# Softmax scale folded into the query copies, minima as biases, head norms by twos, and a new spread of the modulation products, in a two-layer hybrid attention kernel

## The chip, the cores and the metric

The kernel runs on one core of a Trainium2 chip. The metric is the device time of one execution in microseconds (us). The engines are PE (TensorE, matmul), DVE (VectorE), ACT (ScalarE), POOL (GpSimd) and SP (SyncE, which issues the DMAs here). Each engine takes its own instructions in the order in which they stand in its queue and waits where an operand is not there yet.

## The reference

Two trunk layers work on 640 tokens (512 latent, 128 context) of width 1024, all in float32. What is computed in each layer, cut to what matters here:

```python
mod = silu(cond) @ ada_w + ada_b                   # two conditions: context, latent
shift, scale, gate = split(mod, 3)
h = rmsnorm(x, norm_g) * (1 + scale) + shift
c_q, c_kv, k_rope, cb, cc, cx, dq, dk, dv, z = split(h @ w_in)
# latent attention, 4 heads: softmax((q . k) * 96**-0.5) @ v, low-rank q and k, v
# short convolution:         cb * conv3(cc * cx)
# differential attention, 4 heads with two softmax maps of width 64 each:
s = einsum(q, k) * 64 ** -0.5                      # q, k with rotary positions
p = softmax(s)
o = rmsnorm((p[0] - lam * p[1]) @ v, subln) * (1 - lambda_init)
mix = concat(o_mla, o_conv, o_diff) * silu(z)
x = x + gate * (mix @ w_out)
```

Latent queries see 512 latent and 128 cached context keys; context queries see the 128 context keys alone. A final norm and the keys and values of the context tokens are outputs too.

## The kernel before, in words

Activations lie transposed (features on partitions, 640 tokens along the free side) and are worked on in two halves of 320 tokens, j = 0 and 1. A float32 matmul is done as three matmuls over a high and a low part of each operand (`mm3`, lines 362 to 364: high x high, high x low, low x high). The low parts are subtractions on DVE (`mx` L274 for the output projection, `hl` L394 for the layer's input, `klz` L573, `plm` L905 and others) or, for some weights, on POOL (`wli`, L326).

Inside a layer, four sources of work are advanced in step, and the kernel's Python code writes them out in that order; a scheduler then sets each engine's queue from this program order and from what is ready. `main()` yields the projections of the layer one piece at a time; `units()` yields the attention, one unit for each head and block of 128 queries (u = 4 is the context block, then 0 to 3), first the four differential heads, then the four latent (MLA) heads; `bg` holds small jobs (splitting weights, rotary positions); `side()` yields the modulation products. `adv(n)` takes n pieces of `main()`, counts them in `cnt`, and takes one piece of `side()` whenever `cnt` is over a start value and divisible by a step.

**Attention unit (differential, L604 to L650).** PE writes the scores of both maps into PSUM (`S`, two buffers of two banks each, L614). DVE takes the maximum of each row (L624) and multiplies it by minus the scale (L625). ACT computes exp(scale x score + bias) with the row sums (`E`, L631). DVE takes a reciprocal (L633), builds the factor of the second map (L634) and subtracts the maps (L636). PE transposes the result (`tpd`, L594), ACT copies it back (L596), PE multiplies with the values (`O`, L645). The MLA unit is alike with one map (L886, L887, L889, L891, L892). Query copies out of PSUM are ACT copies (L530 for the differential queries, L807 for the latent ones). After a head, `diff_norm` (L651 to L662) takes its five root mean squares in ten small DVE operations of 128x5 (L655 on, `rsqrt`) and one of 128x640 (L661).

**Modulation products.** `mod` needs a matrix-vector product for two conditions. One piece of `ada_cols` (L144) loads 128 rows of the transposed weights (`at`, 256 KB, DMA issued by SP) and runs two DVE multiply-reduce operations over 128x512 (`jk`, L153), each with a short read of its sum. The vector silu(cond), half of it at a time, lies broadcast in a single buffer `cb2`; `silu_bcast` (L134) fills it by two DMAs, a tanh on ACT (L140) and two DVE operations (L141, L142). In layer 0, `side()` has 48 pieces: step 0 the first half of layer 0's gate; step 1 the second half of that gate and of layer 1's shift and scale; step 2, after a new broadcast, the first half of layer 1's shift and scale. Step 2 is 32 products. In layer 1 there are 16 pieces, 32 products, for its gate.

**Output projection (`out_half`, L1149).** Sixteen halves (eight output tiles, two token halves), each of eight steps of three matmuls. In the order of the code: tiles 0 to 3 with both halves, tiles 4 to 7 with the first half, then everything left of `side()`, then the norm of the first half (`y_n`, L203), the second half of tiles 4 and 5, and, between the second halves of tiles 6 and 7, the modulated input of the next layer (`t`, L373, on DVE; `hh`, L390, on ACT; `hl`, L394). The first matmuls of layer 1 (`p1qk`) read `hh` and `hl`, and `t` reads layer 1's scale, `mod_1`.

The two places that set the spread of the products before:

```python
QD, QM, SIDE0 = 5, 3, 18
C1, C2 = 44, 126
SIDES = (8, 4, 5)
...
                cnt[0] += 1
                if cnt[0] > SIDE0 and cnt[0] % SIDES[0 if cnt[0] < C1 else 1 if cnt[0] < C2 else 2] == 0:
                    next(sg, None)
...
                if m % 2 == 0:            # in out_half, for m in range(8)
                    next(sg, None)
```

## Time and profile before

| what | value |
| --- | --- |
| three timed runs | 832.89, 837.35, 837.39 us (median 837.35) |
| the profiled execution, its own time | 832.23 us |
| its span in the trace | 830.2 us |
| PE busy | 783.8 us, 94% |
| DVE busy | 633.4 us, 76% |
| ACT busy | 445.8 us, 54% |
| POOL busy | 70.0 us, 8% |
| mean granted TensorE clock | 0.992 |

The span is the part of the execution that the trace covers; 2.0 us lie around it. A busy share is a mean over stages: layer 0's attention runs from about 80 to 374 us, its output projection to 433, layer 1's attention to 759, and its output projection to the end. The rows below are read stage by stage.

### The profile page before, as it was taken

The page shows a single profiled execution, that of the slowest core. Times are in us where ns is not written, and L with a number is a line of the kernel's source. Part 1 is how long each engine was busy: PE and PEld are TensorE (multiplying, and loading weights), DVE is VectorE, ACT ScalarE, POOL GpSimd, SP SyncE. Part 2 cuts the span into 40 slices and gives each one's busy share as a digit, 9 for nine tenths or more (in the row PEclk, how much of TensorE's full clock was granted, in tenths as well). Part 3 has the DMA queues.
Part 4 walks back from the last instruction along what each step waited for, and adds up shares of the span by engine and source line. Part 5 has one row for each costly group of instructions (what it writes and reads, how often), then busy time and mean ns, then how long its engine had stood idle before and what let it go on. Part 6 is the DMA issues. An engine that isn't in the chain of part 4 may idle for free.

```text
span 830.2 us, 14320 instructions
## 1 busy us (share of the span) xinstructions
PE 783.8 (94%) x5390; PEld 739.3 (89%) x5390; DVE 633.4 (76%) x1494; ACT 445.8 (54%) x978; POOL 70.0 (8%) x45
## 2 busy tenths in 40 slices
PE   6999999989999899999999999999999899999994
PEld 1389988989999888999999998899999899899994
DVE  4788989989998778789567778987778556668535
ACT  2255447454747667674334545546557667756310
POOL 3300011030001102000220002003000200200000
PEclk9999999999999999999999999999999999999997
DMA  8916434132420322135620433411111001111503
GB/s 311 386 66 197 131 104 135 44 92 71 157 83 27 107 90 83 45 120 184 240 102 22 154 103 109 143 30 58 51 59 52 26 26 52 51 53 50 179 1 126
DMA packets 66164, 85.52 MB, mean 103 GB/s; under 512 B 4976, under 2 KB 47408, under 8 KB 66096
## 3 DMA queue, kind: packets, MB, share of 16 engines
q1 hardware_dynamic: 65520, 83.96, 30.9%
q8 instruction: 42, 0.69, 0.3%
q10 hardware_dynamic: 576, 0.66, 0.2%
q14 instruction: 26, 0.21, 0.1%
HBM read 78.14 MB, written 6.46 MB: 102 GB/s over the span
## 4 chain that ended last, share of the span: by engine, by line
PE 60%; DVE 18%; ACT 9%; DMA 7%; issue 3%; POOL 1%; SPq 1%; POOLq 0%; DVEq 0%; ACTq 0%
PE wo L363 5%; PE wo L362 4%; PE wo L364 4%; DVE jk L153 4%; DVE sm L624 2%; ACT E L631 2%; PE O L645 2%; PE p1c L362 2%; PE p1c L364 2%; PE p1c L363 2%; PE tpm L900 2%; PE p1qk L363 2%; PE p1qk L362 2%; PE S L614 2%; PE p1qk L364 2%
## 5 line engine op out<-in xcount | busy, mean ns | idle before, releaser
L153 DVE CUSTOM_DVE_ANT_0 jk<-at,cb 128x512 bf16<-128x512 f32 x128 | 91.9, 718 | 4.9 <-DMA at<-in_adaT 4.2
L631 ACT ACTIVATE E<-S,sm 128x640 f32<-128x640 f32 (+1 forms) x80 | 56.0, 706 | 61.4 <-DVE sm L625 43.3
L363 PE MATMUL wo<-mx,who 128*128 128x320 f32 x256 | 79.3, 311 | 0.1
L364 PE MATMUL wo<-mx,wlo 128*128 128x320 f32 x256 | 79.0, 309 | 0.0
L362 PE MATMUL wo<-mx,who 128*128 128x320 f32 x256 | 78.5, 310 | 0.0
L624 DVE TENSOR_REDUCE sm<-S 128x1 f32<-128x640 f32 (+1 forms) x80 | 55.3, 711 | 3.4 <-PE S L615 2.4
L889 ACT ACTIVATE Em<-Sm,smm 128x640 f32<-128x640 f32 (+1 forms) x40 | 28.3, 708 | 41.9 <-DVE smm L887 40.5
L236 ACT ACTIVATE sqn<-xn 128x320 f32<-128x320 f32 x32 | 15.1, 471 | 64.8 <-DVE xn L1164 64.5
L363 PEld LDWEIGHTS wo<-mx,who 128*128 128x128 f32 x256 | 48.1, 188 | 0.8 <-DVE mx L274 0.6
L614 PE MATMUL S<-kh,qs 128*128 128x320 f32 x128 | 40.7, 327 | 8.5 <-ACT E L631 8.4
L364 PEld LDWEIGHTS wo<-mx,wlo 128*128 128x128 f32 x256 | 48.1, 188 | 0.0
L362 PEld LDWEIGHTS wo<-mx,who 128*128 128x128 f32 x256 | 47.8, 188 | 0.0
L362 PE MATMUL v<-whi_dv,hh 128*128 128x272 f32 x160 | 46.3, 289 | 0.0
L363 PE MATMUL v<-wli_dv,hh 128*128 128x272 f32 x160 | 46.0, 288 | 0.0
L364 PE MATMUL v<-whi_dv,hl 128*128 128x272 f32 x160 | 46.0, 288 | 0.0
L645 PE MATMUL O<-v,atd 128*128 128x128 f32 x336 | 44.1, 275 | 0.2 <-ACT atd L596 0.2
L1164 DVE SCALAR_TENSOR_TENSOR xn<-wo,mod,xn 128x320 f32<-128x320 f32 (+2 forms) x48 | 19.6, 435 | 31.2 <-PE wo L364 21.4
L645 PEld LDWEIGHTS O<-v,atd 128*128 128x128 f32 x336 | 42.1, 192 | 0.5 <-ACT atd L596 0.5
L363 PE MATMUL p0qk<-hl,whi_qk 128*128 128x320 f32 x128 | 40.2, 315 | 2.4 <-DVE hl L394 2.4
L326 POOL TENSOR_TENSOR wli_c<-ri_c,whi_c 128x1024 fp32r<-128x1024 f32 x8 | 19.8, 2475 | 264.7 <-PE p0zm L363 85.4
L362 PE MATMUL p1c<-hh,whi_c 128*128 128x320 f32 x128 | 41.6, 325 | 0.0
L362 PE MATMUL p0c<-hh,whi_c 128*128 128x320 f32 x128 | 41.2, 322 | 0.0
(377 smaller groups left out, 2660.6 us busy)
## 6 DMA issues: line engine op xcount, KB each, us to landing
at<-in_adaT SPq DMA_DIRECT2D x64, 256.0 KB, 4.0
ada<-in_adaA SPq DMA_DIRECT2D x32, 256.0 KB, 5.1
ri_qk<-in_wi SPq DMA_DIRECT2D x16, 512.0 KB, 4.8
ri_c<-in_wi SPq DMA_DIRECT2D x16, 512.0 KB, 4.0
ro<-in_wo SPq DMA_DIRECT2D x16, 512.0 KB, 4.4
ri_dv<-in_wi SPq DMA_DIRECT2D x8, 544.0 KB, 4.6
ri_zd<-in_wi SPq DMA_DIRECT2D x8, 512.0 KB, 3.7
x<-in_xT SPq DMA_DIRECT2D x16, 160.0 KB, 4.8
```

The source lines that it names most:

```text
L153: V.tensor_tensor_reduce(out=junk, in0=raw, in1=cb2[:, c, :], scale=1.0, scalar=0.0, op0=ALU.mult, op1=ALU.add, accum_out=acc)
L326: eng.tensor_tensor(out=lo, in0=raws[hf], in1=hi.bitcast(F32), op=ALU.subtract)
L362: TE.matmul(ps, ah, bh, start=first, stop=False)
L363: TE.matmul(ps, ah, bl, start=False, stop=False)
L364: TE.matmul(ps, al, bh, start=False, stop=last)
L614: TE.matmul(ps[:, j, 0:HB], qs[:, a, qc], kh[:, a, js], start=True, stop=False)
L624: V.tensor_reduce(out=sm[:, a:a + 1], in_=Sv[a], axis=AX.XY if u < 4 else AX.X, op=ALU.max)
L631: S.activation(ev, Sv[a], AF.Exp, bias=sm[:, 2 + a:3 + a], scale=DIFF_SCALE, accum_out=so)
L645: TE.matmul(po[:, 0:128], at[:, c * 128:(c + 1) * 128], vv[:, h * 128:(h + 1) * 128], start=c == 0, stop=c == n - 1)
L889: S.activation(e if u < 4 else e[:, 0:128], Sv, AF.Exp, bias=sm[:, 1:2], scale=MLA_SCALE, accum_out=sm[:, 2:3])
L900: TE.transpose(tp[:, c * 128:(c + 1) * 128], toktile(e, c), ident)
L1164: V.scalar_tensor_tensor(out=xn[kt][:, a:e], in0=ps[:, a - j * HB:e - j * HB], scalar=mod[l][2][:, kt, c:c + 1], in1=xn[kt][:, a:e], op0=A ...
```

## The change: what it does

1. **Scale.** The copies of the query projections out of PSUM (L530, L807 of before) become ACT activations with scale = -(softmax scale). The scores then have the other sign: DVE takes the minimum, ACT computes exp(-score + minimum). The multiplications L625 and L887 (40 each) go. L634 takes a column of `neglam` as a tensor operand in place of a scalar operand.
2. **Head norms by twos.** The sums of two heads lie side by side and `diff_norm` runs once for both: ten small operations of 128x10 instead of twice ten of 128x5. The output tile of the even head waits for that of the odd one. `flush` finishes at most one head at a time.
3. **Spread.** While attention runs, a piece of `side()` is taken when `cnt` is over 18 and divisible by 10 in layer 0, over 128 and divisible by 10 in layer 1. In the output projection one piece is taken for each half (m == 0) in place of four. What is left is drained at the same place in the code, after the twelfth half.

DVE's queue goes from 1476 instructions to 1356; the numbers of matmuls, ACT and POOL instructions and DMAs stay. The diff, without the parts that only rename:

```diff
-    QD, QM, SIDE0 = 5, 3, 18
-    C1, C2 = 44, 126
-    SIDES = (8, 4, 5)
+    QD, QM = 5, 3
+
+    SIDES = ((18, 10), (128, 10))
...
+        def copy(dst, src, scale=None):
+            if scale is None:
+                S.copy(dst, src)
+            else:
+                S.activation(dst, src, AF.Copy, scale=scale)
...
-            res["qr"] = q = yield from proj_raw(nm, 0)
+            res["qr"] = q = yield from proj_raw(nm, 0, -DIFF_SCALE)
...
             for a in range(2):
-                V.tensor_reduce(out=sm[:, a:a + 1], in_=Sv[a], axis=AX.XY if u < 4 else AX.X, op=ALU.max)
-            V.tensor_scalar(out=sm[:, 2:4], in0=sm[:, 0:2], scalar1=-DIFF_SCALE, scalar2=None, op0=ALU.mult)
+                V.tensor_reduce(out=sm[:, a:a + 1], in_=Sv[a], axis=AX.XY if u < 4 else AX.X, op=ALU.min)
...
-                S.activation(ev, Sv[a], AF.Exp, bias=sm[:, 2 + a:3 + a], scale=DIFF_SCALE, accum_out=so)
+                S.activation(ev, Sv[a], AF.Exp, bias=sm[:, a:a + 1], scale=-1.0, accum_out=so)
...
-            V.tensor_scalar(out=sm[:, 7:8], in0=s0[:, u:u + 1], scalar1=sm[:, 6:7], scalar2=neglam[:, l:l + 1],
-                            op0=ALU.mult, op1=ALU.mult)
+            V.scalar_tensor_tensor(out=sm[:, 7:8], in0=s0[:, k5:k5 + 1], scalar=sm[:, 6:7], in1=neglam[:, l:l + 1],
+                                   op0=ALU.mult, op1=ALU.mult)
...
-        def diff_norm(h, acc):
+        def diff_norm(h, oss, ss, s0):
...
-            V.scalar_tensor_tensor(out=e[:, 5:10], in0=ss[:, 0:5], scalar=1.0 / 128, in1=e[:, 0:5], op0=ALU.mult,
+            V.scalar_tensor_tensor(out=e[:, 10:20], in0=ss[:, 0:10], scalar=1.0 / 128, in1=e[:, 0:10], op0=ALU.mult,
                                    op1=ALU.add)
-            y = rsqrt(e[:, 5:10], 5, "d" + tg)
-            ov = os_.rearrange("p (u d) -> p u d", u=5)
-            V.tensor_tensor(out=ov, in0=ov, in1=y.unsqueeze(2).to_broadcast([P, 5, P]), op=ALU.mult)
-            return os_
+            y = rsqrt(e[:, 10:20], 10, "d" + tg)
+            for k, os_ in enumerate(oss):
+                ov = os_.rearrange("p (u d) -> p u d", u=5)
+                V.tensor_tensor(out=ov, in0=ov, in1=y[:, 5 * k:5 * k + 5].unsqueeze(2).to_broadcast([P, 5, P]),
+                                op=ALU.mult)
...
-                    S.copy(qp[m][:, js], ps)
+                    copy(qp[m][:, js], ps, -MLA_SCALE)
...
-            V.tensor_reduce(out=sm[:, 0:1], in_=Sv, axis=AX.XY if u < 4 else AX.X, op=ALU.max)
-            V.tensor_scalar(out=sm[:, 1:2], in0=sm[:, 0:1], scalar1=-MLA_SCALE, scalar2=None, op0=ALU.mult)
+            V.tensor_reduce(out=sm[:, 0:1], in_=Sv, axis=AX.XY if u < 4 else AX.X, op=ALU.min)
...
-                if cnt[0] > SIDE0 and cnt[0] % SIDES[0 if cnt[0] < C1 else 1 if cnt[0] < C2 else 2] == 0:
+                if cnt[0] > SIDES[l][0] and cnt[0] % SIDES[l][1] == 0:
                     next(sg, None)
...
-            while waiting and waiting[0][2] in r and (cnt[0] > waiting[0][4] + 3 or done):
+            n = 0
+            while waiting and waiting[0][2] in r and (n == 0 and cnt[0] > waiting[0][4] + 3 or done):
+                n += 1
...
-                if m % 2 == 0:
+                if m == 0:
                     next(sg, None)
```

Counted in DVE's queue, the 128 products stand in these stages, before and after: ahead of layer 0's first attention unit 8 and 6; between the differential heads of layer 0 52 and 22; between its MLA heads 31 and 16; in its output projection 5 and 52 (20 between the halves, then the 32 of step 2); in layer 1 up to its second differential head 32 and 0; heads three and four 0 and 6; MLA heads 0 and 12; at the end of layer 1's attention and among the `mx` subtractions 0 and 14.

The first place is DVE's queue where layer 0's output projection ends. Before, the chain of the norm ends (`y_n`), the last residual sums (`xn`) follow, and `t_0_0` is the first step of layer 1's input:

```order
L202 SCALAR_TENSOR_TENSOR w_n_0_4846<-w_n_0_4846,v_n_0_4843 128x3
L203 SCALAR_TENSOR_TENSOR y_n_0_4845<-w_n_0_4846,y_n_0_4845 128x3
L1164 SCALAR_TENSOR_TENSOR xn_5_4720<-wo_4873,mod_2_105,xn_5_4720 128x192
L1164 SCALAR_TENSOR_TENSOR xn_5_4720<-wo_4873,mod_2_105,xn_5_4720 128x128
L373 SCALAR_TENSOR_TENSOR t_0_0_4914<-xn_0_4394,mod_1_107,rb_n_0_4904 128x320
L245 TENSOR_TENSOR sqn_10_4490<-sqn_10_4490,sqn_15_4900 128x320
L373 SCALAR_TENSOR_TENSOR t_0_1_4919<-xn_1_4493,mod_1_107,rb_n_0_4904 128x320
L394 SCALAR_TENSOR_TENSOR hl_0_4913<-t_0_0_4914,mod_0_106,hh_0_4912 128x320
L373 SCALAR_TENSOR_TENSOR t_0_2_4925<-xn_2_4553,mod_1_107,rb_n_0_4904 128x320
```

After, the new broadcast (`tb`, `cb`) and all 32 products of step 2 stand between `y_n` and `t_0_0`; 31 of them stand in the place marked by the dots, with the sums of tiles 5 to 7, two sums of squares and five small steps that finish `mod_0` and `mod_1` between them:

```order
L141 TENSOR_SCALAR tb_4625<-tb_4625 128x1024
L203 SCALAR_TENSOR_TENSOR y_n_0_4775<-w_n_0_4776,y_n_0_4775 128x3
L142 TENSOR_TENSOR cb_109<-cb_109,tb_4625 128x1024
L1180 SCALAR_TENSOR_TENSOR xn_5_4531<-wo_4803,mod_2_105,xn_5_4531 128x192
L153 ISA jk_4631,mod_0_106<-at_4629,cb_109 128x512
L153 ISA mod_0_106 128x1
...
L164 SCALAR_TENSOR_TENSOR mod_1_107<-mod_1_107,small_in 128x16
L373 SCALAR_TENSOR_TENSOR t_0_0_4844<-xn_0_4178,mod_1_107,rb_n_0_4834 128x320
L373 SCALAR_TENSOR_TENSOR t_0_1_4849<-xn_1_4262,mod_1_107,rb_n_0_4834 128x320
L394 SCALAR_TENSOR_TENSOR hl_0_4843<-t_0_0_4844,mod_0_106,hh_0_4842 128x320
```

What moved is step 2, from layer 1's attention to ahead of the first `t`. On PE nothing moved there: the last matmuls `wo` are followed by the first `p1qk`, with nothing between them. On SP the two loads of `cb` and then the 16 loads of `at` stand ahead of the loads of layer 1's first weights, whose low parts POOL subtracts.

The second place is DVE's queue where layer 1's output projection begins. Before, seven `mx` subtractions stand ahead of the last attention output (`osm`, L921):

```order
L689 SCALAR_TENSOR_TENSOR z1c_8647<-z1c_8647,p1c_8648 128x320
L274 TENSOR_TENSOR mx_8748<-mff_6227,mx_8748 128x320
...
L274 TENSOR_TENSOR mx_8766<-mff_7743,mx_8766 128x320
L921 TENSOR_TENSOR osm_8172<-Om_3_3_8719,osm_8172 64x256
L274 TENSOR_TENSOR mx_8769<-mff_7743,mx_8769 128x320
L667 SCALAR_TENSOR_TENSOR osm_8172<-osm_8172,z1zm_7519 128x640
L689 SCALAR_TENSOR_TENSOR z1c_8647<-z1c_8647,p1c_8706 128x320
L274 TENSOR_TENSOR mx_8772<-osm_7550,mx_8772 128x320
L950 TENSOR_TENSOR z1c_8647<-z1c_8647,yg_8501 128x640
```

After, `osm` (now L928) comes first, then four products among the last gate operations, and only then the first `mx`, with a product behind each:

```order
L928 TENSOR_TENSOR osm_7980<-Om_3_3_8541,osm_7980 64x256
L153 ISA jk_8574,mod_2_108<-at_8570,cb_109 128x512
...
L675 SCALAR_TENSOR_TENSOR osm_7980<-osm_7980,z1zm_7303 128x640
L153 ISA jk_8578,mod_2_108<-at_8576,cb_109 128x512
...
L697 SCALAR_TENSOR_TENSOR z1c_8463<-z1c_8463,p1c_8528 128x320
L153 ISA jk_8580,mod_2_108<-at_8576,cb_109 128x512
...
L957 TENSOR_TENSOR z1c_8463<-z1c_8463,yg_8320 128x640
L153 ISA jk_8584,mod_2_108<-at_8582,cb_109 128x512
...
L274 TENSOR_TENSOR mx_8608<-mff_6549,mx_8608 128x320
L153 ISA jk_8586,mod_2_108<-at_8582,cb_109 128x512
...
L274 TENSOR_TENSOR mx_8611<-mff_6549,mx_8611 128x320
```

What moved is the first `mx`, from ahead of the last attention output to behind it and four products (a fifth stands behind the first `mx`, and so on to the seventh). On PE the first matmuls `wo` that need only high parts are four; the fifth needs this `mx`.

The third place is DVE's queue at the first latent query block of layer 0's first head, before:

```order
L624 TENSOR_REDUCE sm_0_0_1056<-S_0_0_1057 128x1
...
L624 TENSOR_REDUCE sm_0_0_1056<-S_0_0_1062 128x1
...
L625 TENSOR_SCALAR sm_0_0_1056<-sm_0_0_1056 128x2
L153 ISA jk_1043,part<-at_1041,cb_109 128x512
...
L153 ISA jk_1045,part<-at_1041,cb_109 128x512
...
L633 RECIPROCAL sm_0_0_1056<-sm_0_0_1056 128x1
L634 TENSOR_SCALAR sm_0_0_1056<-s_0_1019,sm_0_0_1056,neglam 128x1
L636 SCALAR_TENSOR_TENSOR E_0_0_1070<-E_0_0_1072,sm_0_0_1056,E_0_0_1070 128x640
```

and after:

```order
L632 TENSOR_REDUCE sm_0_0_1043<-S_0_0_1044 128x1
L632 TENSOR_REDUCE sm_0_0_1043<-S_0_0_1049 128x1
L640 RECIPROCAL sm_0_0_1043<-sm_0_0_1043 128x1
L641 SCALAR_TENSOR_TENSOR sm_0_0_1043<-s_0_1012,sm_0_0_1043,neglam 128x1
L643 SCALAR_TENSOR_TENSOR E_0_0_1056<-E_0_0_1058,sm_0_0_1043,E_0_0_1056 128x640
L632 TENSOR_REDUCE sm_0_1_1107<-S_0_1_1108 128x1
```

What moved: the multiplication L625 is gone from between the row extremes and the exponential, and two products no longer stand between the exponential and the reciprocal.

## Rows read from the trace of the kernel before

**Rows 1.** The page, part 1: busy time, share of the span, instructions.

```profile
PE 783.8 (94%) x5390; PEld 739.3 (89%) x5390; DVE 633.4 (76%) x1494; ACT 445.8 (54%) x978; POOL 70.0 (8%) x45
```

**Rows 2.** Busy time by stretch: bounds, length, busy time (x instructions), PEclk, DMA share, GB/s.

```profile
80.00:265.00 185.00, 176.67 (x1262) 171.37 (x1261) 168.91 (x412) 107.50 (x267) 12.34 (x7) 1.00 0.31 100
265.00:374.00 109.00, 103.17 (x713) 98.16 (x712) 84.28 (x208) 71.82 (x145) 10.07 (x4) 1.00 0.28 86
374.00:433.00 59.00, 57.69 (x394) 57.09 (x393) 41.40 (x93) 21.71 (x35) 9.90 (x4) 1.00 0.53 177
480.00:560.00 80.00, 75.94 (x530) 74.11 (x529) 70.50 (x160) 42.16 (x106) 5.60 (x2) 0.98 0.32 100
560.00:640.00 80.00, 78.89 (x567) 76.63 (x566) 62.09 (x144) 50.82 (x125) 6.55 (x5) 1.00 0.19 57
640.00:760.00 120.00, 115.73 (x815) 112.14 (x815) 74.88 (x172) 80.78 (x167) 9.73 (x4) 1.00 0.12 39
```

**Rows 3.** PE's waits: engine, line <- releaser: total us, times, longest.

```profile
PE S L614 <- ACT E L631: 8.4, 6, 3.1
PE tpd L594 <- ACT E L631: 4.7, 4, 2.1
```

**Rows 4.** Two stretches of 20 us with gaps in PE, columns as in the second group.

```profile
160.00:180.00 20.00, 16.89 (x123) 16.19 (x121) 18.70 (x42) 12.47 (x27) 4.98 (x4) 1.00 0.22 70
520.00:540.00 20.00, 18.00 (x118) 17.69 (x117) 18.34 (x54) 10.77 (x28) 0.00 (x0) 0.91 0.43 139
```

**Rows 5.** Groups of DVE's instructions: busy us, mean ns of one, idle time before.

```profile
L153 DVE CUSTOM_DVE_ANT_0 jk<-at,cb 128x512 bf16<-128x512 f32 x128 | 91.9, 718 | 4.9 <-DMA at<-in_adaT 4.2
L142 DVE TENSOR_TENSOR cb<-cb,tb 128x1024 f32<-128x1024 f32 x4 | 9.0, 2258 | 0.1
L625 DVE TENSOR_SCALAR sm<-sm 128x2 f32<-128x2 f32 x40 | 7.6, 189 | 0.4
L887 DVE TENSOR_SCALAR smm<-smm 128x1 f32<-128x1 f32 x40 | 6.0, 150 | 0.7
```

**Rows 6.** Timeline of DVE, products back to back: start us, length us, operation.

```profile
87.57 0.69 DVE L153 CUSTOM_DVE_ANT_0 jk<-at,cb 128x512 bf16<-128x512 f32 x1
...
89.04 0.69 DVE L153 CUSTOM_DVE_ANT_0 jk<-at,cb 128x512 bf16<-128x512 f32 x1
```

**Rows 7.** Timeline of PE where layer 0 ends: first out-projection matmul, first of layer 1.

```profile
373.74 0.31 PE L362 MATMUL wo<-mx,who 128*128 128x320 f32 x1
...
433.40 0.31 PE L362 MATMUL p1qk<-hh,whi_qk 128*128 128x320 f32 x1
```

**Rows 8.** Timeline of DVE at the same end of layer 0.

```profile
423.84 0.16 DVE L203 SCALAR_TENSOR_TENSOR y_n<-w_n,y_n 128x3 f32<-128x3 f32 x1
425.90 0.68 DVE L1164 SCALAR_TENSOR_TENSOR xn<-wo,mod,xn 128x192 f32<-128x192 f32 x2 [1.90 <-PE wo L364]
426.54 0.55 DVE L373 SCALAR_TENSOR_TENSOR t<-xn,mod,rb_n 128x320 f32<-128x320 f32 x1
```

**Rows 9.** The chain that ended last, around a broadcast of the condition.

```profile
119.07 3.98 DMA cb<-in_cond
```

**Rows 10.** One line, all products of layer 0: count, min/median/max ns, first and last start.

```profile
L153 DVE CUSTOM_DVE_ANT_0 jk<-at,cb x74: 673/684/2767, 79.0 to 319.1; 128x512 bf16<-128x512 f32 x74
```

**Rows 11.** Timelines of DVE and PE where layer 1 ends.

```profile
755.50 2.90 DVE L274 TENSOR_TENSOR mx<-mff,mx 128x320 fp32r<-128x320 f32 x7
758.43 0.42 DVE L921 TENSOR_TENSOR osm<-Om,osm 64x256 f32<-64x256 f32 x1
...
760.82 0.82 DVE L950 TENSOR_TENSOR z1c<-z1c,yg 128x640 f32<-128x640 f32 x1
...
759.00 0.31 PE L362 MATMUL wo<-mx,who 128*128 128x320 f32 x1
```

**Rows 12.** Groups of ACT's instructions of 128x320.

```profile
L530 ACT COPY raw0qk<-p0qk 128x320 f32<-128x320 f32 x12 | 5.2, 430 | 4.5 <-PE p0qk L364 4.5
L688 ACT ACTIVATE z0zd<-p0zd 128x320 f32<-128x320 f32 x8 | 3.5, 438 | 1.5 <-PE p0zd L364 1.5
```

More of the change, by code (lines that the diff above doesn't have):

```diff
@@ L88, in small @@
     def small(name, n=16):
-        return smp.tile([P, n], F32, tag="small%d" % n, name=name, bufs=16 if n == 16 else 1)
+        return smp.tile([P, n], F32, tag="small%d" % n, name=name, bufs=16 if n == 16 else 2)
     cond = cst.tile([P, KT, 2], F32, name="cond")
@@ L524, in proj, with proj_raw @@
             return ps
-        def proj_raw(nm, b, js=(0, 1), r=None):
-            r = r or slot("raw%d%s%d" % (l, nm, b))
-            for j in js:
+        def proj_raw(nm, b, scale=None):
+            r = slot("raw%d%s%d" % (l, nm, b))
+            for j in range(2):
                 ps = yield from proj(nm, b, j)
-                S.copy(r[:, j * HB:(j + 1) * HB], ps)
+                copy(r[:, j * HB:(j + 1) * HB], ps, scale)
                 yield
@@ L985, in main @@
                 for b in range(2):
-                    S.copy(raws[b][:, js], ps[b])
+                    copy(raws[b][:, js], ps[b], -DIFF_SCALE if b == 0 else None)
                 if j == 0:
@@ L1064, in units @@
                 tg = "%d_%d" % (l, h)
-                acc = (slot("os" + tg), small("ss" + tg), small("s0" + tg))
+                if h % 2 == 0:
+                    oss, ss, s0 = [], small("ss" + tg), small("s0" + tg)
+                oss.append(slot("os" + tg))
+                acc = (oss[-1], ss, s0)
                 for u in (4, 0, 1, 2, 3):
@@ L1138, in tile_kernel @@
         while "gate" not in r:
-            next(sg)
+            next(sg, None)
         while bg:
```

21 lines of the change are left out of this document (12 added, 9 removed).

## The prediction

> **What bounds the kernel now.** The page's first part [rows 1] says that PE is the bound: it is busy 783.8 of 830.2 us, DVE 633.4. An average hides where PE's missing time is, so I read the busy time stretch by stretch next [rows 2]. In the attention of both layers (80 to 374 us, 480 to 760 us) PE is idle for 185.00 - 176.67 = 8.33, 5.83, 4.06, 1.11 and 4.27 us, 23.6 us in sum. That is all that a change of DVE's work can give back there, whatever it removes from DVE. The reader is to see that idle time goes with products: per 100 us it is 4.5 and 5.3 in the two stretches of layer 0 and 5.1 in 480 to 560, which all carry them, and 1.4 in 560 to 640, which carries none; 640 to 760 carries none either and has 3.6. Layer 0's output projection is the other case: PE 57.69 of 59 us, DVE 41.40, so DVE has 17.6 us of room beside matmuls that run without a break. Third come PE's waits [rows 3]: its score matmuls and its transposes wait for the exponential on ACT, 13.1 us in ten waits. The exponential waits for DVE's maximum, and DVE is an in-order queue, so a product that stands ahead of a maximum delays PE. Last I read what happens at the end of layer 0 [rows 7, 8], since the order of instructions changes most there.
>
> **The end of layer 0 (A): a new wait.** Step 2, 32 products, must be done before layer 1's scale is, and the first `t` needs that scale. Before, it was done before the projection had run far. Now four of five products that used to run under attention are taken after it, 20 between the halves and 32 in a row. Where does that row begin? The 16 halves take 433.40 - 373.74 = 59.66 us [rows 7], 3.73 us each, so the twelfth ends at 418.5 and its product, the last that reads the old broadcast, stands at about 415 to 416. The load of `cb` then takes 3.98 us [rows 9] and the tanh, an ACT pass over 1024 columns, at most 3.2 times the 0.438 us of 320 columns [rows 12], 1.4 us: ready at about 421 to 422, before `y_n` ends at 423.84 + 0.16 = 424.00 [rows 8]. The added 15 products between the halves are 15 x 0.735 = 11.0 us of DVE, which the room of 17.6 us hides; if that cover fails, `y_n` comes later by what is missing. One product costs 0.735 us back to back, from two starts that lie two products apart [rows 6]. From 424.00: `cb` 2.26 [rows 5], 32 x 0.735 = 23.5, three sums `xn` of 0.68 [rows 8] 2.0, two sums of squares at the 0.55 of `t`, which has their shape, 1.1, five small steps at the 0.16 of `y_n` 0.8, then `t` 0.55 and `hh` on ACT at 0.44, the price of an ACT pass of this shape [rows 12]. That makes 454.7. PE, which had its first `p1qk` at 433.40 and has nothing else in its queue, stands still for **21.3 us**. With `cb` at the price of two products (1.4) it is 20.4, the lower bound.
>
> Two additions to it. POOL runs four subtractions in this projection, 9.90 us [rows 2]; they come later now, since the loads of those weights stand behind the 16 loads of `at` on SP, and would run beside the products. One product of layer 0 took 2.767 us where the median is 0.684 [rows 10], 2.08 more. Four such would be 8.3, none is the other end; I take three, **6.2 us**, as two instructions in a pair come so close that one may fall between products. [...] Second, the clock. [...] The stretch 160 to 180 had 3.11 us of idle time and kept 1.00. [...] A = 21.3 + 6.2 + 1.8 = **29.3**, from 20.4 to 33.2.
>
> **The end of layer 1 (B).** Before, seven `mx` are done from 755.50 on, 0.41 us each, before the last `osm` at 758.43, and PE starts `wo` at 759.00 without a wait [rows 11]. Now the first `mx` stands behind that `osm` (ends 758.85), four products (2.94), a gate pass of 0.82, one of 0.41 and the `z1c` product of 0.82 [rows 11], and itself takes 0.41: 764.25. PE has four matmuls without it, spaced 59.66 / 384 = 0.155 us [rows 7], to 759.6: it waits 4.65 us. Then each of seven `mx` has a product behind it, 0.41 + 0.735 = 1.145 us, and feeds six matmuls, 0.93 us: 7 x 0.215 = 1.5. B = **+6.1**. If the chain of the last head ends earlier by what attention gains on DVE alone it could be 2; if the 12 products that now stand in the latent heads delay it, 8.
>
> **The start of layer 0 (C).** Two products fewer stand before the first unit (-1.5), but the first broadcast, `cb` 2.26 with the scaling ahead of it, which I put at one product (0.735), now stands among the subtractions that the last matmuls of the first pass wait for: up to +3.0. Matmuls of the values are there to cover most of it: **+0.5**.
>
> **Attention (D).** Products: those between layer 0's heads fall from 83 to 38, 54%. Their stretches idle 14.16 us in 294, 4.8 per 100; the stretches without products idle 5.38 in 200, 2.7 per 100. 0.54 x 2.1 x 2.94 = -3.3. In layer 1, the 32 products of step 2 leave the first two heads: 480 to 560 goes from 5.1 to the 1.4 of the next stretch, -2.9; the 18 that enter later give +1.0. That is -5.2. The folded multiplications are 7.6 + 6.0 = 13.6 us of DVE [rows 5] and the 40 operations saved by norms at the 0.189 of a small one another 7.6. Products bought 6.2 us for 45 + 32 = 77 of 0.735, 56.6 us: 0.11 us of PE for each us of DVE. So 21.2 us are worth -2.3. Beyond its load, each L625 sits in the path from a maximum to the exponential for which PE waits: ten waits, 0.19 each plus the hand-over between two operations, put at 0.06: -2.5. D = **-10**. The least is the folded path alone, -2.5; the most is all the idle time, 23.6, with the 1.8 of the clock: -25.4. I stay near the lower end because the row of 640 to 760 shows that idle time remains where no product stands. L634 with a tensor operand changes nothing that I can price: 0, as it stands behind the exponential beside PE's queue.
>
> **ACT.** 28 query copies go from 0.430 to 0.438 us [rows 12], 0.2 us beside an engine at 54%: +0.2 at most.
>
> **The sum.** 29.3 + 6.1 + 0.5 - 10 + 0.2 = +26.1. Against the profiled execution's own 832.23 us this is 858.3. The fastest timed run, 832.89, agrees with that execution; the two others lie 5.1 above it, and no row says which a median will be. I add half of it, 2.5: **861 us**, against a median of 837.35 before. A measurement of this kernel tells about 1% (8 us) from no change.
>
> **The rivals.** *Within 1%: relief pays for the gap.* If all idle time in attention comes from DVE's queue, D is -25.4. With the other terms as above that gives 832.2 + 36.1 - 25.4 = 843, still 1.3% above; with POOL and clock at nothing, 835. The place is the maxima of L624 and L886; it decides in favour of "not slower" once relief exceeds some 20 us while the gap stays at its lower bound. For it speaks that the waits for the exponential are the largest; against it, that 640 to 760 idles 4.27 us without products, and that relief and gap are bought with the same 52 products, one by one hidden and now 32 not hidden at all. 837 us with the half difference, chance 0.12. Faster by over 1% needs more than all idle time there is: 0.02.
>
> *The change doesn't relieve anything.* PE's idle time follows from the length of the chain maximum, exponential, subtraction and the two score buffers, not from the load: then D is -2.5 and the time 866 + 2.5 = 868. For it: 640 to 760. Chance 0.15.
>
> *The clock stays low.* [...] If it is twice that, another 3.6 us and also 3.6 after the wait in B: about 865, chance 0.08. [...]
>
> **Chances and range.** The forecast has 0.63. Lower end: relief at -20 with POOL at 2 us gives 832.2 + 36.1 - 4.2 - 20 + 2.5 = 846.6, rounded down to 845; upper end: the second rival with POOL at 8.3 and B at 8, 872, rounded up to 874. Outside lie the first rival and the tails. Faster by over 1%: 0.03; within 1%: 0.10; slower by over 1%: 0.87.
>
> **What the profile of the changed kernel would show.** A is right if PE has one gap of 20 to 28 us between the last `wo` and the first `p1qk` of layer 1, with some 32 products in a row on DVE and the first `t` behind them, a few of them over 2 us beside POOL. B is right if PE waits 4 to 5 us for the first `mx` of layer 1. D is right if PE's idle time in attention falls from 23.6 to about 14 us. What would make it wrong: a first `t` that doesn't wait for step 2, or attention stretches that become free of idle time.

## The result, and the profile after

The changed kernel takes **859.68 us** (median of 4 runs, 859.27 to 860.59) against 837.37 (4 runs, 832.89 to 838.68): a ratio of 1.0283, with a 95% interval of 1.0257 to 1.0309. The forecast was 861, slower. The profiled execution takes 860.59 us, 28.4 us over that of before, with a span of 858.8, 28.6 us over; it is these two executions that are compared below.

PE is still busy nearly all the time, DVE a little less than before (page, part 1, of after, as [rows 1]):

```profile
PE 791.2 (92%) x5390; PEld 745.9 (87%) x5390; DVE 624.8 (73%) x1374; ACT 448.1 (52%) x978; POOL 72.6 (8%) x45
```

The stretches of after, with the columns of [rows 2], cut at the same events in layer 0 and within some 5 us of them in layer 1; the fourth lies between the last matmul of layer 0's output projection and the first of layer 1:

```profile
80.00:262.00 182.00, 180.07 (x1292) 175.72 (x1290) 143.03 (x304) 108.51 (x268) 14.04 (x8) 1.00 0.24 77
262.00:371.00 109.00, 101.30 (x690) 96.50 (x691) 71.14 (x160) 69.75 (x140) 9.29 (x4) 0.98 0.20 64
371.00:429.00 58.00, 57.46 (x394) 57.13 (x393) 47.70 (x124) 15.22 (x27) 0.00 (x0) 1.00 0.67 226
429.40:457.70 28.30, 0.11 (x1) 0.00 (x0) 27.41 (x59) 5.93 (x7) 10.96 (x4) 0.56 0.45 157
...
505.00:585.00 80.00, 79.97 (x575) 78.51 (x574) 55.12 (x94) 48.44 (x115) 6.94 (x4) 1.00 0.18 55
585.00:665.00 80.00, 80.00 (x582) 79.03 (x581) 63.90 (x138) 50.52 (x125) 4.72 (x4) 1.00 0.21 66
665.00:783.00 118.00, 114.12 (x787) 107.76 (x785) 79.55 (x177) 76.97 (x156) 10.88 (x4) 1.00 0.23 73
```

Idle time of PE in attention is now 1.93 + 7.70 + 0.03 + 0.00 + 3.88 = 13.5 us, where it was 23.6. In the fourth stretch PE does nothing for 28.3 us. The waits of PE name what it waits for, there and at the end of layer 1:

```profile
PE p1qk L362 <- ACT hh L390: 28.3, 1, 28.3
...
PE wo L363 <- DVE mx L274: 2.5, 2, 1.9
...
PE wo L362 <- DVE z1c L697: 1.5, 1, 1.5
```

On DVE the same place reads as follows, to be held against [rows 8]. `y_n` ends at 421.14, then come `cb` and the products. Two products and two additions of 128x16 take 2.3 to 2.7 us each, and the first `t` starts at 456.57:

```profile
420.99 0.15 DVE L203 SCALAR_TENSOR_TENSOR y_n<-w_n,y_n 128x3 f32<-128x3 f32 x1
421.11 1.23 DVE L142 TENSOR_TENSOR cb<-cb,tb 128x1024 f32<-128x1024 f32 x1
...
434.23 2.71 DVE L153 CUSTOM_DVE_ANT_0 jk<-at,cb 128x512 bf16<-128x512 f32 x1
...
436.98 2.72 DVE L153 CUSTOM_DVE_ANT_0 jk<-at,cb 128x512 bf16<-128x512 f32 x1
...
439.74 2.33 DVE L1040 TENSOR_TENSOR mod<-mod,part 128x16 f32<-128x16 f32 x1
...
442.60 2.43 DVE L161 TENSOR_TENSOR mod<-mod,small_in 128x16 f32<-128x16 f32 x1
...
455.94 0.17 DVE L1040 TENSOR_TENSOR mod<-mod,part 128x16 f32<-128x16 f32 x1
...
456.57 1.01 DVE L373 SCALAR_TENSOR_TENSOR t<-xn,mod,rb_n 128x320 f32<-128x320 f32 x2
```

POOL's four subtractions lie beside the four long ones:

```profile
434.04 5.11 POOL L326 TENSOR_TENSOR wli_qk<-ri_qk,whi_qk 128x1024 fp32r<-128x1024 f32 x2 [111.77 <-ACT whi_qk L324]
439.13 5.87 POOL L326 TENSOR_TENSOR wli_dv<-ri_dv,whi_dv 128x1088 fp32r<-128x1088 f32 x2
```

Behind the gap the granted clock is 0.50 in the first of these windows, in which DVE is busy 5.19 of 5.30 us; it is 0.94 in the second and 0.72 in the third (windows of after, columns as in [rows 2]):

```profile
457.70:463.00 5.30, 5.24 (x19) 5.15 (x20) 5.19 (x12) 3.61 (x8) 0.00 (x0) 0.50 0.01 3
463.00:469.00 6.00, 5.42 (x36) 5.16 (x35) 3.25 (x11) 1.82 (x5) 0.00 (x0) 0.94 0.00 0
469.00:475.00 6.00, 5.30 (x30) 5.30 (x31) 4.89 (x19) 2.13 (x6) 0.00 (x0) 0.72 0.00 0
```

At the end of layer 1 PE begins its output projection and waits twice; the first `mx` starts at 785.36 on DVE (timelines of PE and of DVE, to be held against [rows 11]):

```profile
783.53 0.42 PE L362 MATMUL wo<-mx,who 128*128 128x320 f32 x1 [1.53 <-DVE z1c L697]
785.89 0.63 PE L363 MATMUL wo<-mx,who 128*128 128x320 f32 x1 [1.95 <-DVE mx L274]
```

```profile
785.36 0.48 DVE L274 TENSOR_TENSOR mx<-mff,mx 128x320 fp32r<-128x320 f32 x1
...
786.37 0.48 DVE L274 TENSOR_TENSOR mx<-mff,mx 128x320 fp32r<-128x320 f32 x1
```

Cut at the first score matmul, the first `wo`, the first `p1qk` and the last `wo` of each layer (starts on PE's timeline), the two executions compare like this, in us:

| stage | before | after | difference |
| --- | --- | --- | --- |
| start to the first score matmul | 89.5 | 90.6 | +1.1 |
| layer 0, attention | 284.2 | 280.1 | -4.1 |
| layer 0, output projection | 59.5 | 58.4 | -1.1 |
| gap to the first matmul of layer 1 | 0.1 | 28.6 | +28.5 |
| layer 1, first projections to the first score matmul | 47.3 | 52.4 | +5.1 |
| layer 1, attention | 278.3 | 271.2 | -7.1 |
| layer 1, output projection | 58.1 | 64.3 | +6.2 |

The sum is +28.6, the difference of the spans. The attention stages gain 11.2 us, and three places lose 39.8.

### The profile page after: what moved, and what is told of

Its sections match the earlier page's. It is cut to its first block, busy times and chain, and to the rows that moved or that the text cites. A ratio compares the mean times of both kernels' runs of the same rounds, so it can differ in the third digit from the quotient of the medians.

```text
span 858.8 us, 14162 instructions
## 1 busy us (share of the span) xinstructions
PE 791.2 (92%) x5390; PEld 745.9 (87%) x5390; DVE 624.8 (73%) x1374; ACT 448.1 (52%) x978; POOL 72.6 (8%) x45
## 4 chain that ended last, share of the span: by engine, by line
PE 64%; DVE 15%; DMA 10%; ACT 5%; issue 3%; SPq 1%; POOL 1%; DVEq 0%; ACTq 0%; POOLq 0%
DVE jk L153 4%; PE O L652 4%; DMA at<-in_adaT 4%; PE wo L363 3%; PE wo L364 3%; PE wo L362 3%; PE v L362 2%; PE p1qk L362 2%; PE v L363 2%; PE p1qk L363 2%; PE v L364 2%; PE p1qk L364 2%; PE S L621 2%; PE S L622 2%; PE p0qk L363 2%
## 5 line engine op out<-in xcount | busy, mean ns | idle before, releaser
L363 PE MATMUL wo<-mx,who 128*128 128x320 f32 x256 | 80.0, 315 | 2.5 <-DVE mx L274 2.5
L362 PE MATMUL wo<-mx,who 128*128 128x320 f32 x256 | 79.6, 314 | 1.5 <-DVE z1c L697 1.5
L362 PE MATMUL p1qk<-hh,whi_qk 128*128 128x320 f32 x128 | 41.3, 328 | 28.3 <-ACT hh L390 28.3
L363 PEld LDWEIGHTS wo<-mx,who 128*128 128x128 f32 x256 | 49.0, 192 | 3.0 <-DVE mx L274 3.0
L362 PEld LDWEIGHTS wo<-mx,who 128*128 128x128 f32 x256 | 48.8, 192 | 1.8 <-DVE z1c L697 1.8
L362 PEld LDWEIGHTS p1qk<-hh,whi_qk 128*128 128x128 f32 x128 | 24.9, 197 | 28.6 <-ACT hh L390 28.5
L363 PE MATMUL v<-wli_dv,hh 128*128 128x272 f32 x160 | 46.9, 293 | 0.0
L896 ACT ACTIVATE Em<-Sm,smm 128x640 f32<-128x640 f32 (+1 forms) x40 | 28.3, 709 | 34.9 <-DVE smm L894 29.6
L326 POOL TENSOR_TENSOR wli_c<-ri_c,whi_c 128x1024 fp32r<-128x1024 f32 x8 | 22.2, 2777 | 267.0 <-PE p0zm L363 84.5
```

Of the source, the lines that this page charges most:

```text
L326: eng.tensor_tensor(out=lo, in0=raws[hf], in1=hi.bitcast(F32), op=ALU.subtract)
L362: TE.matmul(ps, ah, bh, start=first, stop=False)
L363: TE.matmul(ps, ah, bl, start=False, stop=False)
L896: S.activation(e if u < 4 else e[:, 0:128], Sv, AF.Exp, bias=sm[:, 0:1], scale=-1.0, accum_out=sm[:, 2:3])
```

## The experiments

Times of runs are medians; each ratio is against runs of the kernel before on the same chip, whose medians there were 836.23, 835.65 and 835.37 us. Stages are read as in the table above, from one execution of each kernel; since runs of before alone lie between 832.5 and 841.9 us, differences of a stage under 2 or 3 us are not built on.

**1. The spread alone** (`spread_only`): the kernel before with

```diff
-    SIDES = (8, 4, 5)
+    SIDES = ((18, 10), (128, 10))
...
-                if m % 2 == 0:
+                if m == 0:
                     next(sg, None)
```

> The kernel before with nothing but the new spread. If the spread makes the loss: the gap before layer 1's first matmul is 27 to 30 us, and the time 862 to 866 us, that is 859.7 plus the 2 to 6 us that the folded scale and the norms by twos are worth. Rival: those are worth nothing, 859 to 861. If the loss came from the other edits: near 837.

Measured: 864.10 us, 1.0343 (1.0309 to 1.0377). PE waits 28.1 us for the first `hh` of layer 1 and 3.3 us at the end of layer 1, as with the whole change. The spread makes the loss, and more than the loss; the other edits give back 4.4 us beside it (859.68; the times of the two sets of runs do not overlap, the intervals of their ratios touch).

**2. Everything but the spread** (`fold_norms_old_spread`): the changed kernel with the two lines above turned back.

> The changed kernel with the old spread of the products (steps 8, 4, 5 and four pieces in each half of the output projection); folded scale, minima and norms by twos stay. If the spread makes all of the loss, the gaps of 28.3 us at the end of layer 0 and 3.5 us at the end of layer 1 are gone and only the relief of fewer DVE operations is left: 831 to 835 us, against 837.4 before. Rival: the relief in attention came from the thinner products alone, so this one stays within 1 us of before (837). Second rival: the longer-lived output tiles and pairwise norms cost something that the spread hid: above 840.

Measured: 835.56 us over 12 runs, 0.9995 (0.9976 to 1.0014). The first rival holds: 120 fewer DVE operations are worth nothing that shows, with the old spread. The gaps at the ends of the layers are gone. What stands against a gain is read from PE's longest wait (its timeline, then DVE's in the same place, then ACT's and POOL's):

```profile
130.42 0.41 PE L621 MATMUL S<-kh,qs 128*128 128x320 f32 x1 [4.54 <-ACT E L638]
```

```profile
121.13 1.23 DVE L142 TENSOR_TENSOR cb<-cb,tb 128x1024 f32<-128x1024 f32 x1
122.28 3.03 DVE L579 TENSOR_TENSOR klz<-kf,hk 64x640 fp32r<-64x640 f32 x1
125.23 0.67 DVE L153 CUSTOM_DVE_ANT_0 jk<-at,cb 128x512 bf16<-128x512 f32 x1
...
126.80 0.69 DVE L153 CUSTOM_DVE_ANT_0 jk<-at,cb 128x512 bf16<-128x512 f32 x1
...
127.82 0.69 DVE L153 CUSTOM_DVE_ANT_0 jk<-at,cb 128x512 bf16<-128x512 f32 x1
...
128.43 0.29 DVE L632 TENSOR_REDUCE sm<-S 128x1 f32<-128x128 f32 x1
128.63 0.68 DVE L153 CUSTOM_DVE_ANT_0 jk<-at,cb 128x512 bf16<-128x512 f32 x1
...
129.24 0.29 DVE L632 TENSOR_REDUCE sm<-S 128x1 f32<-128x128 f32 x1
```

```profile
129.56 0.37 ACT L638 ACTIVATE E<-S,sm 128x128 f32<-128x128 f32 x1 [2.23 <-DVE sm L632]
```

```profile
121.39 3.24 POOL L326 TENSOR_TENSOR wli_qk<-ri_qk,whi_qk 128x1024 fp32r<-128x1024 f32 x1 [12.50 <-ACT whi_qk L324]
```

A new broadcast (`cb`), a `klz` that takes 3.03 us instead of 0.82 beside a subtraction of POOL, and four products stand ahead of the second minimum, at 129.24; the exponential starts behind it, and PE waits 4.54 us. Shortening each unit by 0.2 us does not touch such a pile. The attention of layer 0 takes 291.1 us here against 284.2 in the profiled execution of before, that of layer 1 275.1 against 278.3.

The 6.9 us in layer 0 are for the most part not standstill but, by an estimate, the clock (layer 0's attention of before, of this run, and of run 5 below, columns as in [rows 2]):

```profile
89.54:373.74 284.20, 270.04 (x1897) 259.92 (x1896) 243.87 (x592) 175.03 (x395) 22.41 (x11) 1.00 0.29 92
```

```profile
89.98:381.04 291.06, 276.05 (x1897) 266.94 (x1897) 232.65 (x531) 177.64 (x395) 22.73 (x11) 0.97 0.29 90
```

```profile
90.81:379.82 289.01, 275.38 (x1896) 265.08 (x1896) 229.53 (x515) 177.47 (x395) 22.64 (x11) 0.98 0.28 87
```

PE idles 15.0 us instead of 14.2, but its granted clock is 0.97 instead of 1.00: 0.03 x 291 is some 8 to 9 us, an estimate. The clock is low where PE's three longest waits of this stage end, of 4.54 us (at 130.4), 2.60 (at 262.0) and 2.64 (at 335.9): it is 0.50 from 131 to 134, 264 to 270 and 336 to 342. Before, with a longest wait of 3.11 us in the stage, it is 1.00. That these waits brought the clock down is what their places suggest; no run tests it by itself.

**3. Which of the two edits is worth the 4.4 us** (`fold_new_spread`): the changed kernel with `diff_norm`, its small tiles and `flush` as before.

> The changed kernel with norms head by head as before, that is the folded scale and the new spread. The spread alone gave 864.1 us, all three edits 859.7. If the folded scale, which shortens the path from the row extremes to the exponential, is what is worth the 4.4 us: 859 to 861. Rival: the norms by twos are (40 small operations fewer): 863 to 865. In between if both.

Measured: 860.13 us, 1.0273 (1.0216 to 1.0331). So the folded scale accounts for the gain and the norms by twos change nothing that can be told (860.13 against 859.68, from two sets of runs). The size is less sure than that: the times of this run and of run 1 do not overlap, but they come from two chips, and the intervals of the two ratios overlap.

**4. Layer 1's products early** (`l1_products_early`):

```diff
-    SIDES = ((18, 10), (128, 10))
+    SIDES = ((18, 10), (40, 11))
```

> The changed kernel, with layer 1's 32 gate products taken from count 40 on at every eleventh count, so that all stand ahead of the first subtraction for the output projection; layer 0 as changed. Theory: the wait and the slow clock at the end of layer 1 (5.6 us against before) go, and 0.11 us per us of DVE come back in the heads: 854 to 856 us. Rival: the wait there is set by the last attention output and not by the products, and the time stays at 859 to 860.

Measured: 853.37 us, 1.0205 (1.0175 to 1.0234), a little under the theory's range. Layer 1's output projection is back at 58.0 us, its attention takes 273.1 (after: 271.2). So the end of layer 1 is worth 6.3 us of the loss, as theory had it.

**5. Both layers' products early** (`both_early`):

```diff
-    SIDES = ((18, 10), (128, 10))
+    SIDES = ((18, 5), (40, 11))
```

> As the run with layer 1's products early, and layer 0's products at every fifth count, so that step 2 is done ahead of the norm that ends layer 0. Theory: the gap of 28.3 us and the slow clock after it go as well, some 3 to 4 us of relief in layer 0 are given back: 829 to 834 us, faster than before. Rival: the relief came from the thin spread in attention alone; then 836 to 838.

Measured: 835.15 us over 12 runs, 0.9977 (0.9957 to 0.9997). The gap is gone, and so is nearly all that attention had gained in layer 0: 289.0 us. The theory's 829 to 834 was too low: PE idles 13.6 us in this stage, and the granted clock is 0.98 (the third row under run 2), which costs some 6 us by an estimate, 0.02 x 289.

**6. Without step 2** (`no_step2`): the changed kernel without the 32 products and their broadcast in layer 0. It leaves out the first half of the sums for layer 1's shift and scale, and it adds a broadcast in layer 1, for the gate there.

```diff
-                if step > 0 or l == 0:
+                if step < 2:
                     silu_bcast(hf, "%d%d" % (l, step))
...
-                    for k2 in range(4):
-                        yield from ada_cols(ll, s, hf, k2, first)
+                    if step < 2:
+                        for k2 in range(4):
+                            yield from ada_cols(ll, s, hf, k2, first)
```

> The changed kernel with the 32 products of step 2 and their broadcast left out (the first half of the sum for layer 1's shift and scale is not computed; one broadcast is added in layer 1 for its gate). If the gap is made by these products alone, PE's gap ahead of layer 1's first matmul goes from 28.3 us to under 3 us, and with the slow clock behind it (some 4 us) the time is 826 to 830 us. Rival: behind the products stands another wait of about the same end (the norm, or the low parts of the first weights on POOL), and the gap stays over 6 us: above 834.

Measured: 836.15 us, 1.0005 (0.9983 to 1.0027). The gap is gone (0.1 us) and the first projections take 46.9 us, so these products make it. But the time is that of the rival, without the gap that the rival named: layer 0's output projection takes 64.8 us, 6.4 more than after, and layer 1's attention, which has the added broadcast, 275.9, 4.7 more. In the projection another wait came up, at the sums of squares for the norm (PE's timeline), behind products between the halves, of which one waits 1.24 us for its own load (DVE's). The granted clock of this stage is 0.95, some 3 of the 6.4 us by an estimate:

```profile
420.45 1.44 PE L212 MATMUL st_n<-ones,sqn 128*128 128x1 f32 x6 [3.87 <-DVE sqn L245]
```

```profile
414.14 0.69 DVE L153 CUSTOM_DVE_ANT_0 jk<-at,cb 128x512 bf16<-128x512 f32 x1 [1.24 <-DMA at<-in_adaT]
...
419.91 0.89 DVE L245 TENSOR_TENSOR sqn<-sqn,sqn 128x320 f32<-128x320 f32 x2 [0.28 <-ACT sqn L236]
```

**7. The subtractions of layer 1's first weights on DVE** (`splits_on_dve`):

```diff
-            unit_q.append((..., G if l > 0 and u < 2 or UNITS[u] in PU else V))
+            unit_q.append((..., G if l > 0 and 0 < 0 or UNITS[u] in PU else V))
```

> The changed kernel with the four subtractions for layer 1's first weights on DVE in place of POOL. If a product beside a POOL subtraction is blocked for 2.0 us (two products and two small steps stood 8.5 us longer in the gap), the gap loses 8.5 us and gains four subtractions of 1.2 us: 24.7 us, and the time is 855 to 857 us. Rival: the long products have another reason (the loads), they stay long, and the gap grows by the four subtractions to 33 us: 863 to 865.

Measured: 855.64 us, 1.0238 (1.0208 to 1.0268). The longest of the 32 products takes 0.694 us (line view of this stretch), the four subtractions 1.22 to 1.28, and PE's wait is 24.2 us:

```profile
L153 DVE CUSTOM_DVE_ANT_0 jk<-at,cb x32: 676/691/694, 422.9 to 451.4; 128x512 bf16<-128x512 f32 x32
```

The long products come from POOL's subtractions beside them: without these none is long.

**8. The gap filled with idle matmuls** (`gap_filled`):

```diff
         out_half(7, 1)
+        if l == 0:
+            fill = bank2("fill").rearrange("p (j c) -> p j c", j=2)[:, :, 0:HB]
+            wf = unit(base + NU + 3)[0][0]
+            for k in range(176):
+                TE.matmul(fill[:, k % 2], wf[:, k % 4, 0:128], mix[k % 8][k % 2][0], start=True, stop=True)
```

> The changed kernel with 176 idle matmuls of 320 columns (their result is not used) between the last matmul of layer 0 and the first of layer 1. They take 23.5 to 26 us of the gap of 28.3. If the low clock behind the gap costs time (0.50 in the first 5 us, 0.90 in 47 us), the clock stays at its higher level there and the time falls by 3 to 5 us to 855 to 857, though the kernel does more work. Rival: the first pass is paced by DVE (two operations of 0.46 us for each step), so the clock costs nothing there: 859 to 860.

Measured: 862.58 us (858.64 to 867.68), 1.0324 (1.0283 to 1.0365): no gain, the rival's side. The profiled execution, 867.68, is the slowest of the four. The granted clock is 1.00 through the filled 25.6 us, and 0.68 and 0.65 in the first projections all the same (windows, columns as in [rows 2]):

```profile
434.00:459.60 25.60, 25.60 (x176) 25.35 (x174) 25.01 (x51) 5.42 (x5) 10.84 (x4) 1.00 0.50 169
462.60:468.00 5.40, 4.59 (x18) 4.11 (x18) 5.31 (x12) 3.68 (x7) 0.00 (x0) 0.68 0.00 0
468.00:474.00 6.00, 3.39 (x14) 3.42 (x15) 3.67 (x14) 0.92 (x2) 0.00 (x0) 0.65 0.00 0
```

PE gets a `hh` and a `hl` only every 0.92 us there and is short of work, and a gap of 3.0 us was left ahead of it. The stretch to the first score matmul takes 54.8 us (after: 52.4), at a mean granted clock of 0.91 as in after, and PE idles 3.4 us in it (after: 1.3). So this fill does not buy the 5.1 us back; what they are made of is taken up below.

**9. A spread between** (`thin_and_done`): `SIDES = ((18, 6), (40, 11))`.

> The changed kernel with a spread between the two: layer 0's products at every sixth count and one piece in each half of its output projection, which leaves two products behind the twelfth half; layer 1's gate from count 40 on at every eleventh. Theory: no gap at either end of a layer, and 12 fewer products between the heads of layer 0 than with every fifth count: 830 to 834 us, below before by 0.3 to 0.8%. Rival: the last broadcast and products stand behind the norm as before and leave a gap of a few us: 836 to 840.

Measured: 837.86 us over 12 runs, 1.0018 (0.9997 to 1.0038). No gap ahead of layer 1, but layer 0's output projection takes 64.9 us, with a wait of 4.2 us for the sums of squares as in run 6, and its attention 289.0. The rival was nearer, though not for its reason.

**10. Layer 0's products later** (`later_in_layer0`):

```diff
-    SIDES = ((18, 10), (128, 10))
+    SIDES = ((18, 8, 4), (40, 11, 11))
...
-                if cnt[0] > SIDES[l][0] and cnt[0] % SIDES[l][1] == 0:
+                if cnt[0] > SIDES[l][0] and cnt[0] % SIDES[l][1 if cnt[0] < 136 else 2] == 0:
...
-                if m == 0:
+                if m % 4 == 0:
```

> The changed kernel with layer 0's products every eighth count in the differential heads, every fourth in the latent heads, and two pieces in each half of the output projection (done after some six halves); layer 1's gate from count 40 on at every eleventh. Theory: idle time in the differential heads goes with products (8.3 us before, 1.9 with the thin spread), that in the latent heads does not (5.8 before with 31 products, 7.7 with 16), so that moving products from the first to the second gains: layer 0's attention takes 284 to 286 us from the first score matmul on, against 289.0 with every fifth count, and the time is 830 to 833 us. Rival: DVE, 71 of 109 us busy there with 16 products, becomes the bound of the latent heads with 46: 836 to 840.

Measured: **824.33 us** (821.57 to 825.03), 0.9836 (0.9798 to 0.9874): faster than both kernels, and by more than expected; layer 0's attention takes 277.2 us. The ratio holds the folded scale and layer 1's early products too; run 5 (835.15) has both and differs in layer 0's spread alone. Its windows, columns as in [rows 2]:

```profile
80.00:262.00 182.00, 178.92 (x1280) 174.28 (x1279) 153.75 (x333) 109.84 (x269) 14.54 (x9) 1.00 0.28 86
262.00:374.00 112.00, 107.24 (x734) 101.27 (x735) 89.79 (x215) 73.92 (x148) 7.92 (x3) 1.00 0.33 100
374.00:434.00 60.00, 56.16 (x370) 55.87 (x369) 48.44 (x113) 19.76 (x31) 9.96 (x4) 0.94 0.57 194
```

PE idles 3.08 us in the differential heads and 4.76 in the latent ones, at a granted clock of 1.00; DVE, 90 of 112 us busy there, does not become the bound. Of the 11.8 us between the attention of layer 0 here and in run 5, 6.4 are idle time of PE (13.6 and 7.2) and most of the rest is the clock, 0.98 there (some 6 us by the estimate under run 5) and 1.00 here. What is left to gain is in the output projection, 64.9 us: PE waits 3.84 us for the sums of squares, and in DVE's queue ahead of them stands a wait of 3.57 us for the load of a residual (`xn`):

```profile
417.16 1.44 PE L212 MATMUL st_n<-ones,sqn 128*128 128x1 f32 x6 [3.84 <-DVE sqn L245]
```

```profile
412.56 0.55 DVE L1180 SCALAR_TENSOR_TENSOR xn<-wo,mod,xn 128x320 f32<-128x320 f32 x1 [3.57 <-DMA xn<-in_xT]
```

That this wait is the cause is read from the queue; an earlier load was not tried.

**11. One broadcast fewer** (`one_broadcast_less`): run 5 with the first half of all three sums first.

```diff
-            for step, (hf, parts) in enumerate((((0, ((l, 2),)), (1, ((l, 2), (l + 1, 0), (l + 1, 1))),
-                                                 (0, ((l + 1, 0), (l + 1, 1))))) if l + 1 < DEPTH else
-                                               ((0, ((l, 2),)), (1, ((l, 2),)))):
+            every = ((l, 2), (l + 1, 0), (l + 1, 1)) if l + 1 < DEPTH else ((l, 2),)
+            for step, hf in enumerate((0, 1) if l == 0 else (1, 0)):
+                parts = every
...
-                    first = not (step == 2 or step == 1 and (ll, s) == parts[0] and ll == l)
+                    first = step == 0
```

> The run with both layers' products early, with side() in another order: in layer 0 the first half of all three sums, then the second half; in layer 1 the second half first. That needs three broadcasts of the condition in place of four, and the products stay as many. With the old spread and with every fifth count PE's longest waits in the differential heads (4.5 us at 126, 2.5 us at 128) stand behind a broadcast and the products after it. Theory: the early broadcast moves to the last differential head, that wait goes, 831 to 834 us. Rival: the wait moves along with the broadcast and the time stays at 835.

Measured: 830.31 us over 12 runs, 0.9925 (0.9897 to 0.9952), just under the theory's range. No wait of over 2 us is left before 250 us; one of 2.6 stands at 254.

**12. Both** (`later_one_less`): runs 10 and 11 together.

> The two edits of the last two runs together. If both gain: 827 to 831 us, 0.6 to 1% below before. If neither: 835 to 838.

Measured: 829.80 us, 0.9902 (0.9864 to 0.9940): the two do not add up, it is slower than run 10 alone. Layer 0's attention takes 282.2 us, with a wait of 2.6 us in the latent heads (at 324) that run 10 does not have. The stage idles 9.1 us against 7.2 in run 10, and its granted clock is 0.99; why the waits fall so in this order was not followed up.

## Why the prediction was right, point by point

**The gap (A).** The step held, with its place and its reason: forecast 21.3 + 6.2 = 27.5 us of standstill, measured 28.26. Run 6 shows that the 32 products make it. Two errors inside the term cancel in part. `cb` took 1.23 us, not 2.26: the price was a mean over two operations of 1.2 and two of 3.3 us, and the two long ones (at 125.8 and 515.7 in before) stand beside a subtraction of POOL. What was lost beside POOL was 2.02 + 2.03 + 2.16 + 2.26 = 8.5 us (each of the four long operations less its usual 0.69 or 0.17), just over the upper end of 8.3 and not the 6.2 taken; run 7 shows that POOL is the reason. That one of the four subtractions would fall between products was my estimate; each had a long operation beside it. The long product of [rows 10], at 107.67 in before, has a subtraction of POOL beside it too, from 107.09 to 109.89.

**The clock (also A) was mis-sized for the execution compared.** Forecast +1.8, measured +5.1 in the first projections. No run shows the 1.8 that stands in A's sum, nor the 3.6 in its upper end of 33.2, as what the clock costs behind such a gap (the most for D, -25.4, has the 1.8 too); in their place a granted clock of 0.50, 0.94 and 0.72 was measured in the first 17 us behind the gap. The whole stretch can be set beside that of run 4, which has the same gap (columns as in [rows 2]):

```profile
457.76:510.20 52.44, 51.15 (x355) 50.48 (x355) 33.80 (x77) 25.51 (x56) 0.00 (x0) 0.91 0.15 44
```

```profile
459.76:509.49 49.73, 48.45 (x354) 47.78 (x354) 34.93 (x81) 25.69 (x56) 0.00 (x0) 0.97 0.17 51
```

PE idles 1.3 us in both, so DVE's pace is the same; I had left out that all of the first pass's `t` and `hl` now stand behind the products, which is what these 1.3 us are (before: 0.1). What differs is the clock: 0.09 x 52.4 = 4.7 us in after and 0.03 x 49.7 = 1.5 us in run 4, both estimates. Runs 1 and 3, with 0.96, take 50.0 and 50.2 us. So the clock cost 1.5 to 4.7 us behind the same gap, by these estimates: 1.5 in run 4 and 0.04 x 50 = 2.0 in runs 1 and 3, near the 1.8, and 4.7 in after; run 7 took 52.1 us behind a gap of 24.2. Run 8 gained nothing: behind its fill the clock fell again, to 0.91 over the stretch, and PE idled 3.4 us.

**The end of layer 1 (B).** Forecast +6.1, measured +6.2; run 4 gives 6.3 when the products are taken away. The total is right by luck. The wait is 1.53 + 1.95 = 3.5 us, less than the 4.65 of the sum, and a pair of a product and a `mx` takes 1.01 us, not 1.145, so that seven cost 0.6 and not 1.5. The rest goes with the granted clock, 0.61 in this window of after, which B did not have:

```profile
783.00:790.00 7.00, 4.52 (x16) 4.29 (x17) 7.00 (x22) 3.70 (x11) 0.00 (x0) 0.61 0.60 198
```

By an estimate, 0.39 x 7.0 = 2.7 us, a part of it while PE waited.

**The start of layer 0 (C).** Forecast +0.5, measured +1.1.

**Attention (D).** Forecast -10, measured -4.1 - 7.1 = -11.2. The size was right, the reason only in part. I read idle time as going with products in all stages. With the folded scale it does in layer 0's differential heads: 8.60 us with 52 products there (run 2), 7.05 with 46 (run 5), 3.08 with 32 (run 10), 1.93 with 22 (after). But the count is not all: run 11, with 46 and one broadcast fewer among them, idles 5.43, and the new spread without the folded scale, with 22 (run 1), still 5.15. It does not in the latent heads: 5.83 us before, 7.70 after with half the products, 4.76 in run 10 with more; run 8, whose queue there is that of after, idles 10.31, so executions of one order differ by as much. The row that spoke against me stood in [rows 2], 3.6 per 100 us without any product; taken seriously it points to run 10.

The folded scale was priced at -2.5 for the path and a part of -2.3 for the load; with the new spread it measured -4.0 (864.1 to 860.1), with the old one, together with the norms, nothing. The 0.06 in that -2.5 for the hand-over between two operations was my estimate and no run shows it: in before 0.04 us lie between the end of L633 at 97.96 and the start of L634 at 98.00. A pile in DVE's queue and the clock behind its long waits are what the profile of run 2 shows in place of the gain; that they are the reason is argued, not tested. The norms by twos, part of the -2.3, measured nothing. What the sum left out in attention is the granted clock: 0.97 and 0.98 in layer 0 in runs 2 and 5, 1.00 before and in run 10.

**The sum.** By stages A came out at 28.5 + 5.1 - 1.1 = +32.5 against 29.3, B at +6.2, C at +1.1, D at -11.2: +28.6 against +26.1. That 861 lies within 0.2% of the median is in part luck, since the 2.5 us added for the difference between runs of before have nothing to do with the change and filled most of what the sum lacked.

**Statements that were wrong.** The part on the change ahead of the prediction says that step 2 moved there from layer 1's attention, and the prediction that layer 1's first two heads lose step 2. Step 2 was done in layer 0 before; what leaves layer 1's first heads is its gate's 32 products. The counts and terms are those of the right products. "Four of five products that used to run under attention" is wrong as well: of 83 between layer 0's heads 45 moved, as the part on attention counts them. And the chances of faster and of within 1% are given twice, as 0.02 and 0.12 and as 0.03 and 0.10.

**The rivals.** Relief that pays for the gap did not happen: the gain is 11.2 us against 39.8. "Doesn't relieve anything" was right for the latent heads alone. "The clock stays low" happened in the execution compared, behind the gap and around the waits in B: 4.7 us and some 2.7 by the estimates above. Its 865 was not reached because B's other terms came out smaller, attention gained more, and the 2.5 us for the runs of before did not come. The difference of 5.1 us between runs of before did not carry over: runs of after lie within 1.3 us, and half of it was added for nothing (858.3 without it, 860.59 measured in the profiled execution).

## What to carry to other kernels

Work that is moved off the critical stretch has to end somewhere: before thinning a background chain, find what reads its last result and count how much of it stands ahead of that reader in its engine's queue. Here 32 products and a broadcast stood ahead of the first `t`, and PE stood still for 28.3 us; two of these products took 2.71 and 2.72 us instead of 0.69, each beside a subtraction of POOL. Ask per stage whether idle time goes with the background work; here products cost little in the latent heads and several us in the differential ones, and placing them by that took 835.15 us (run 5) to 824.33 (run 10), 1.3%, where removing 120 operations was worth nothing that shows with the old spread and some 4 us with the new one. Look at the granted clock of each stage beside the idle time: of what run 10 gained on run 5 in layer 0's attention, about half is clock by the estimate.
